# Hybrid decoder trunk on one core: a fourth query buffer, other background rates, weight conversion in instructions of 1,024 columns

## The chip, the core and the metric

The kernel runs on one core of one Trainium2 chip. A core has five engines that matter here: TensorE (PE) multiplies matrices into PSUM, VectorE (DVE) and ScalarE (ACT) do element-wise work, GpSimd (POOL) does element-wise work in SBUF, and SyncE (SP) issues most of the DMAs. Each engine takes its own instructions in order; engines wait for each other through semaphores. The metric is the device time of one execution in microseconds, as the median of several runs. Before the change it was 1137.51 us (three runs, 1137.13 to 1138.04).

## What is computed

A decoder trunk of two layers over 512 tokens with 1,024 features: a gated short convolution and an MLP, then one shared key/value projection, then native sparse attention with 16 heads in four groups, and a second MLP. What the change touches is the attention:

```python
def nsa_attention(q, gates, k_cmp, v_cmp, k_sel, v_sel, k_win, v_win, rel_bias):
    ...
    def one_block(qb):                     # 4 blocks of 128 queries
        ...
        logit_c = einsum('bqghd,bngd->bqghn', qt, k_cmp) + bias_c      # 31 compressed keys
        p_c = softmax(where(valid_c, logit_c, NEG_INF)) * has_any
        o_c = einsum('bqghn,bngd->bqghd', p_c, v_cmp)
        ...
        logit_s = einsum('bqghd,bqgkd->bqghk', qt, ks) + bias_s        # selected keys
        o_s = einsum('bqghk,bqgkd->bqghd', softmax(logit_s), vs)
        ...
        logit_w = einsum('bqghd,bkgd->bqghk', qt, kw) + bias_w         # window keys
        o_w = einsum('bqghk,bkgd->bqghd', softmax(logit_w), vw)
        o = gt[..., 0:1] * o_c + gt[..., 1:2] * o_s + gt[..., 2:3] * o_w
```

With 512 tokens the selection takes all eight blocks of 64 keys and the window covers all 512 keys, so both branches attend to all earlier keys. The compressed keys and values come from a small MLP ("phi") over overlapping blocks of 32 tokens.

## The kernel before

All matrices are worked on as 16-bit pairs (a high and a low part), so each product is three matmuls (`mm3`, L341 to L343). Weights come from memory in 32 bit, in pieces of up to 1,024 columns on 128 partitions. `load_piece` issues the DMA of a piece on SP's queue into one of three staging tiles `wst`; `convert_piece` (L171) makes the high part `whi` on ScalarE (L195) and the low part `wlo` on VectorE (L196); `next_piece` takes a piece for use and converts it at once if nobody has. Two pieces are kept converted ahead of the one in use. `convert_piece` has a parameter `step`: with its default of 1,024 a piece is one instruction on each engine, with 512 it is two. In the attention stage `ahead_fine` (L671) calls it with 512 and hands out one half at a time, between the matmuls of a projection.

The attention stage first makes keys, values, gates and the queries of group 0 in one go. Then it runs a list of 96 items. A `Full` item is one group of heads, one block of 128 queries and one branch, with four heads in the first query block, two in the second and one in the third and fourth; 22 items make a head group. A `Cmp` item is the compressed branch of two groups and one query block. Items 0 to 21 belong to group 0, 22 to 43 to group 1, 44 to 69 to group 2 with four `Cmp` items among them (54, 57, 60 and 63), 70 to 95 to group 3 with the other four. An item has five parts which run in later and later steps of the loop, so that several items are under way:

- `st0`: logits on TensorE (L953, L954; L1023, L1024 for `Cmp`), bias and row minimum on VectorE (L961), exponential on ScalarE (L963)
- `st1`, two steps later: transposes on TensorE (L969), high part on ScalarE (L972)
- `st2`, three steps later: low part on VectorE (L975)
- `st3`, four steps later: product with the values (L988 to L990), scaling on VectorE (L906), sums on GpSimd (L908, L911)
- `st4`, six steps later: where a query block is complete, transposes of the output (L922) and its split into the tile `big`

Beside the items runs a generator, `background`, which makes in this order: `raw(0)` (raw keys for phi), `queries(1)`, `phi(0)`, `raw(1)`, `queries(2)`, `phi(1)`, `queries(3)`, and then `out_proj(0)`, the first half of the output projection, once groups 0 and 1 are finished. Each unit is three matmuls of 512 columns (credit 0.65) or six of 155 columns (credit 0.42). In each step of the item loop a credit is added, and units are taken until the credit is used up; a unit of no declared credit counts 0.1. Where an item needs something that is not made yet (`need`), the generator is first run on until it is. What is left over after the last item is run at the end, followed by `out_proj(2)`, the second half, and the second MLP.

A projection accumulates in two PSUM banks `a` (`gated_pair`); `phi` holds the same two banks until its own epilogue has read them. `queries(g)` ends with two multiplications on VectorE into the buffers `at_s` (three, shared with the items' logits), four copies on ScalarE (L742) and four subtractions on GpSimd (L743), which make the tile `Q` of four heads. There are three `Q` tiles, and `queries(3)` writes where group 0 was read; since item 63 is the last reader of group 0, `queries(3)` holds its allocation back until that item has been issued (`cmp0`). `raw` writes its result into `big` by twelve DMAs on SP's queue (L767 to L769).

The program's order on each engine is not quite the order of these calls: the framework orders instructions by its own estimates when it builds the program.

Of the kernel before, what the change touches and what calls it, by code (L numbers as in the profile page):

```python
# [11 lines left out]
F16 = mybir.dt.float16  # L12
# [8 lines left out]
S, D, F, H, G, DH = 512, 1024, 4096, 16, 4, 64  # L21
# [27 lines left out]
def body(ctx, tc, x, rel_bias, norm_mix, norm_mlp, mlp_w1, mlp_w2, a_w_in, a_conv_w, a_w_out,  # L49
# [15 lines left out]
    def bank(tag, shape=(128, 512)):  # L65
        n = {"a": 2, "b": 2, "c": 2, "d": 1, "e": 1}[tag]
        return psum.tile(list(shape), F32, name=tag, bufs=n)
# [78 lines left out]
    def blocked(i):  # L146
        return pieces[i][1] is None
# [23 lines left out]
    def convert_piece(step=1024):  # L171

        i = pos["cv"]
        if i >= len(pieces):
            return
        _, shape, sc = pieces[i]
        t = staged.pop(i)
        pos["cv"] += 1
        if shape is None:
            b = t.rearrange("p (k b n) -> p k b n", k=2, n=128)  # L180
            for e, o, x, y in W_SUMS:
                DVE.tensor_tensor(b[:, :, o], b[:, :, x], b[:, :, y], op=e)  # L182
            hi, lo = (wk[0].tile([128, 2, 7, 128], F16, name=n, bufs=NW2) for n in ("whi2", "wlo2"))
            ACT.activation(hi, b[:, :, 1:], AF.Copy, scale=sc)  # L184
            DVE.scalar_tensor_tensor(lo, b[:, :, 1:], sc, hi, op0=OP.mult, op1=OP.subtract)  # L185
            ready[i] = (hi, lo)
            yield
        else:
            a, n = shape
            hi = wpool.tile([128, PIECE], F16, name="whi", bufs=NW)  # L190
            lo = wpool.tile([128, PIECE], F16, name="wlo", bufs=NW)
            for s in range(0, a * n, step):
                e = min(s + step, a * n)
                w = t[:, s:e]
                ACT.activation(hi[:, s:e], w, AF.Copy, scale=sc)  # L195
                DVE.scalar_tensor_tensor(lo[:, s:e], w, sc, hi[:, s:e], op0=OP.mult, op1=OP.subtract)  # L196
                yield
            r = lambda w: w[:, :a * n].rearrange("p (a n) -> p a n", a=a)
            ready[i] = (r(hi), r(lo))
        while pos["dma"] < len(pieces):  # L200
            like = [j for j in range(pos["cv"], pos["dma"]) if blocked(j) == blocked(pos["dma"])]
            if len(like) >= (NS2 if blocked(pos["dma"]) else NS):
                break
            load_piece()
# [153 lines left out]
    def ftile(name, bufs=2, n=S):  # L358
        return wk[0].tile([128, n], F32, name=name, bufs=bufs)
# [240 lines left out]
    with pool("attn") as ap:  # L600
# [42 lines left out]
        def scaled(ps, rb):  # L643
            t = ftile("at_s", 3)
            DVE.tensor_tensor(t, ps, rb, op=OP.mult)
            return t
# [23 lines left out]

        def ahead_fine():  # L671
            while pos["cv"] < min(pos["use"] + AHEAD, len(pieces)):
                yield from convert_piece(512)


        def keys(br):
# [54 lines left out]

        def queries(g):
            po = yield from gated_pair(xq)
            while g == 3 and "cmp0" not in done:
                yield "wait"
            q = ap.tile([128, 4, S], F16, name="Q", bufs=3)
            for m in range(2):
                t = scaled(po[m], rbq)
                for s in range(2):
                    h, r = 2 * m + s, slice(64 * s, 64 * s + 64)  # L740
                    o = slice(64 - 64 * s, 128 - 64 * s)
                    ACT.activation(q[r, h], t[r], AF.Copy)  # L742
                    POOL.tensor_tensor(q[o, h], t[r], q[r, h], op=OP.subtract)  # L743
                yield
            Qs[g] = q
# [94 lines left out]
        done = set()  # L840
# [40 lines left out]
        for k in (keys(0), keys(1), marked("q0", queries(0)), values(0), values(1), gates()):  # L881
            drain(k)
# [123 lines left out]
        class Cmp:  # L1006
# [7 lines left out]

            def st0(self):
                gp, qb, n = self.gp, self.qb, self.n
                if (gp, qb) == (0, 3):
                    done.add("cmp0")
                s = bank("b")[:, 0:256].rearrange("p (h n) -> p h n", h=8)
                for j in range(8):  # L1020
                    g, h = 2 * gp + j // 4, j % 4
                    q = Qs[g][:, h, qb * 128:(qb + 1) * 128]
                    PE.matmul(s[:, j, :n], q, KC[:, 0, g, :n], start=True, stop=False)  # L1023
                    PE.matmul(s[:, j, :n], q, KC[:, 1, g, :n], start=False, stop=True)  # L1024
                lg = ftile("at_s", 3)[:, 0:256].rearrange("p (h n) -> p h n", h=8)
                i = 8 * qb + 7
                tc_ = TC[gp].rearrange("p g h n -> p (g h) n")
                tv = tc_[:, :, i::-1] if i - n < 0 else tc_[:, :, i:i - n:-1]
                DVE.tensor_tensor(lg[:, :, :n], s[:, :, :n], tv, op=OP.add)
                mx = ap.tile([128, 8], F32, name="c_m", bufs=2)  # L1030
                DVE.tensor_reduce(mx, lg[:, :, :n], axis=mybir.AxisListType.X, op=OP.max)
                DVE.tensor_tensor(lg[:, :, :n], lg[:, :, :n], mx[:, :, None].to_broadcast([128, 8, n]),
                                  op=OP.subtract)
                self.p = ftile("at_p", 3)[:, 0:256].rearrange("p (h n) -> p h n", h=8)
                if n < 32:
                    POOL.memset(self.p[:, :, n:], 0.0)
                ACT.activation(self.p[:, :, :n], lg[:, :, :n], AF.Exp, bias=zero, scale=1.0 / SL)
                self.l = ap.tile([128, 8], F32, name="c_l", bufs=4)
                DVE.tensor_reduce(self.l, self.p[:, :, :n], axis=mybir.AxisListType.X, op=OP.add)
# [76 lines left out]
        credit = 3.0  # L1116
        for i in range(len(items) + 6):
            if i < len(items):
                for k in items[i].need():
                    while k not in done:  # L1120
                        if next(bg, "end") in ("wait", "end"):
                            raise RuntimeError(k)
                at_item.get(i, lambda: None)()
                items[i].st0()
            credit += 0.91 if i < 54 else 0.72 if i < 68 else 0.6
            while credit > 0.0:
                u = next(bg, "end")
                if u in ("wait", "end"):
                    credit = 0.0
                else:  # L1130
                    credit -= u or 0.1
            for s in (1, 2, 3, 4):
                j = i - lead[s]
                if 0 <= j < len(items):
                    getattr(items[j], f"st{s}")()
# [9 lines left out]
    with pool("hidden_b") as hp:  # L1145
# [5 lines left out]
        for half in range(2):  # L1151
            nc.gpsimd.dma_start(fng[half], bass.AP(tensor=final_norm.tensor, offset=final_norm.offset + half * S,
                                                   ap=[[0, 128], [1, S]]))
# [130 lines left out]
```

## Time and profile before

| what | value |
|---|---|
| median of three runs | 1137.51 us |
| the profiled execution | 1136.88 us |
| its span, first to last instruction | 1135.1 us |
| TensorE busy | 1095.8 us, 97% of the span |
| VectorE busy | 832.3 us, 73% |
| ScalarE busy | 568.5 us, 50% |
| GpSimd busy | 157.6 us, 14% |
| mean granted TensorE clock | 0.995 |

A row of a group reads: line of the kernel, engine, operation, output and inputs with their shapes, how often, then busy time in microseconds and the mean duration in nanoseconds, then the idle time of the engine before such instructions and what ended it. A row of the timeline reads: start and duration in microseconds, engine, line, operation, and in brackets the idle time before it and what released it. Matmuls overlap in these records, so the cost of one on a busy TensorE is the distance between two starts, not its duration.

### The profile page before, as it was taken

How to read it: one execution, taken by the hardware profiler on the slowest of the kernel's cores; microseconds unless marked ns; L12 is line 12 of the kernel's file. 1: busy time of each engine (PE TensorE's matmuls, PEld its weight loads, DVE VectorE, ACT ScalarE, POOL GpSimd, SP SyncE). 2: the span in 40 equal slices, each digit the busy share in tenths (PEclk: the TensorE clock that was granted, in tenths of full speed). 3: DMA queues.
4: the chain of work that ended last, by engine and by line, in shares of the span. 5: the costliest groups of instructions: out<-in, count | busy, mean ns of one | idle time of the engine just before them, and what ended most of it. 6: DMA issues, size and time to landing. Idle time of an engine off the chain costs nothing.

```text
span 1135.1 us, 20099 instructions
## 1 busy us (share of the span) xinstructions
PE 1095.8 (97%) x7959; PEld 694.1 (61%) x7959; DVE 832.3 (73%) x1498; ACT 568.5 (50%) x922; POOL 157.6 (14%) x198
## 2 busy tenths in 40 slices
PE   8999999999999999999999989899999999999985
PEld 4444444446884448865767666664444787445874
DVE  4755458765897556999589969896895598754795
ACT  4532235444433444556679777765544433343452
POOL 0000000422000221001002022220122100123020
PEclk9999999999999999999999999999999999999998
DMA  6433335333333333313334341112633333330221
GB/s 210 130 94 97 107 105 172 113 93 113 112 112 112 111 95 107 112 42 120 112 78 122 83 138 38 39 38 74 187 111 112 111 109 115 105 95 7 84 84 75
DMA packets 149378, 115.75 MB, mean 102 GB/s; under 512 B 8612, under 2 KB 146564, under 8 KB 149284
## 3 DMA queue, kind: packets, MB, share of 16 engines
q1 hardware_dynamic: 146736, 109.47, 31.8%
q10 hardware_dynamic: 2260, 4.40, 1.3%
q8 instruction: 62, 1.02, 0.4%
q0 software_dynamic: 288, 0.61, 0.2%
q14 instruction: 32, 0.26, 0.1%
HBM read 110.22 MB, written 2.14 MB: 99 GB/s over the span
## 4 chain that ended last, share of the span: by engine, by line
PE 50%; DVE 19%; ACT 11%; issue 7%; POOL 7%; DMA 5%; SPq 1%; DVEq 0%; ACTq 0%; POOLq 0%
POOL ml_z L503 6%; PE a L341 4%; PE a L342 4%; PE a L343 4%; DVE wlo L185 4%; DMA wst<-mlp_w_dram 3%; ACT rh L504 3%; PE c L343 3%; PE c L342 3%; PE c L341 3%; PE b L342 3%; PE b L341 3%; PE b L343 3%; DVE wlo L196 3%; DVE ml_t L499 2%
## 5 line engine op out<-in xcount | busy, mean ns | idle before, releaser
L195 ACT ACTIVATE whi<-wst 128x1024 f16<-128x1024 f32 (+4 forms) x171 | 142.4, 858 | 127.9 <-PE b L342 38.4
L196 DVE SCALAR_TENSOR_TENSOR wlo<-wst,whi 128x1024 f16<-128x1024 f32 (+4 forms) x171 | 169.9, 1001 | 40.2 <-ACT whi L195 39.9
L503 POOL TENSOR_TENSOR ml_z<-ml_z 128x256 f32<-128x256 f32 x128 | 99.9, 801 | 610.1 <-ACT ml_z L501 410.1
L184 ACT ACTIVATE whi<-wst 128x1792 f16<-128x1792 f32 x64 | 106.9, 1692 | 135.4 <-DVE wst L182 102.3
L341 PEld LDWEIGHTS <-whi 128*128 128x128 f16 x1024 | 100.4, 98 | 112.3 <-issue 5.5
L343 PEld LDWEIGHTS <-wlo 128*128 128x128 f16 x1024 | 100.2, 98 | 112.1 <-issue 0.4
L342 PEld LDWEIGHTS <-whi 128*128 128x128 f16 x1024 | 100.2, 98 | 107.6 <-issue 2.0
L505 DVE TENSOR_TENSOR rl<-ml_z,rh 128x1792 f16<-128x1792 f32 x32 | 64.8, 2026 | 135.9 <-ACT rh L504 135.7
L185 DVE SCALAR_TENSOR_TENSOR wlo<-wst,whi 128x1792 f16<-128x1792 f32 x64 | 128.8, 2019 | 3.0 <-ACT whi L184 2.9
L182 DVE TENSOR_TENSOR wst<-wst 128x256 f32<-128x256 f32 x256 | 108.9, 469 | 24.4 <-DMA wst<-mlp_w_dram 23.4
L504 ACT ACTIVATE rh<-ml_z 128x1792 f16<-128x1792 f32 x32 | 54.3, 1698 | 106.1 <-POOL ml_z L503 106.1
L551 PEld LDWEIGHTS <-whi 128*128 128x128 f16 x896 | 87.7, 98 | 16.2 <-issue 5.6
L552 PEld LDWEIGHTS <-wlo 128*128 128x128 f16 x896 | 87.6, 98 | 15.0 <-issue 4.2
L550 PEld LDWEIGHTS <-whi 128*128 128x128 f16 x896 | 87.7, 98 | 10.5
L343 PE MATMUL b<-xsh,wlo 128*128 128x512 f16 x208 | 78.8, 379 | 0.0
L342 PE MATMUL b<-xsl,whi 128*128 128x512 f16 x208 | 78.8, 379 | 0.0
L341 PE MATMUL b<-xsh,whi 128*128 128x512 f16 x208 | 78.7, 379 | 0.0
L501 ACT ACTIVATE ml_z<-ml_t 128x1024 f32<-128x1024 f32 x32 | 33.8, 1057 | 88.4 <-DVE ml_t L499 88.4
L963 ACT ACTIVATE at_p<-at_s,at_m 128x128 f32<-128x128 f32 (+3 forms) x128 | 71.0, 557 | 13.7 <-DVE at_m L961 12.6
L551 PE MATMUL a<-rl,whi 128*128 128x256 f16 x256 | 69.8, 273 | 3.7 <-DVE rl L505 3.7
L341 PE MATMUL c<-xsh,whi 128*128 128x512 f16 x192 | 72.8, 379 | 0.0
L342 PE MATMUL c<-xsl,whi 128*128 128x512 f16 x192 | 72.8, 379 | 0.0
(309 smaller groups left out, 2686.4 us busy)
## 6 DMA issues: line engine op xcount, KB each, us to landing
wst<-mlp_w_dram SPq DMA_DIRECT2D x256, 256.0 KB, 3.3
wst<-a_w_in_dram SPq DMA_DIRECT2D x18, 512.0 KB, 3.5
wst<-w_kv_dram SPq DMA_DIRECT2D x12, 512.0 KB, 3.5
T<-ext_d ACTq DMA_DIRECT2D x4, 1056.0 KB, 6.0
wst<-a_w_out_dram SPq DMA_DIRECT2D x8, 512.0 KB, 3.4
wst<-b_w_qg_dram SPq DMA_DIRECT2D x8, 512.0 KB, 3.5
wst<-b_w_o_dram SPq DMA_DIRECT2D x8, 512.0 KB, 3.3
wst<-a_w_in_dram SPq DMA_DIRECT2D x8, 384.0 KB, 5.5
```

The source lines that it names most:

```text
L182: DVE.tensor_tensor(b[:, :, o], b[:, :, x], b[:, :, y], op=e)
L184: ACT.activation(hi, b[:, :, 1:], AF.Copy, scale=sc)
L185: DVE.scalar_tensor_tensor(lo, b[:, :, 1:], sc, hi, op0=OP.mult, op1=OP.subtract)
L195: ACT.activation(hi[:, s:e], w, AF.Copy, scale=sc)
L196: DVE.scalar_tensor_tensor(lo[:, s:e], w, sc, hi[:, s:e], op0=OP.mult, op1=OP.subtract)
L341: PE.matmul(ps, w[0], xs[0], start=start, stop=False)
L342: PE.matmul(ps, w[0], xs[1], start=False, stop=False)
L343: PE.matmul(ps, w[1], xs[0], start=False, stop=stop)
L503: POOL.tensor_tensor(z[:, o], z[:, a], z[:, b], op=e)
L504: ACT.activation(rh[0][:, p], z[:, 1:8], AF.Copy)
L550: PE.matmul(acc7[i], wh, xh, start=c == 0 and not other, stop=False, skip_group_check=other)
L551: PE.matmul(acc7[i], wh, xl, start=False, stop=False, skip_group_check=other)
```

## The change

Three things change in the attention stage. There are four `Q` tiles instead of three, and the hold of `queries(3)` until item 63 is gone. `ahead_fine` converts a piece of 1,024 columns in one instruction on each engine instead of two. The credit of each step is set by another table: 1.04 for steps 0 to 41, 0.65 for 42 to 52, 0.68 for 53 to 68 and 0.74 from 69, where it was 0.91 up to step 53, 0.72 up to 67 and 0.6 from 68.

```diff
         def ahead_fine():
             while pos["cv"] < min(pos["use"] + AHEAD, len(pieces)):
-                yield from convert_piece(512)
+                yield from convert_piece()
...
         def queries(g):
             po = yield from gated_pair(xq)
-            while g == 3 and "cmp0" not in done:
-                yield "wait"
-            q = ap.tile([128, 4, S], F16, name="Q", bufs=3)
+            q = ap.tile([128, 4, S], F16, name="Q", bufs=4)
...
             def st0(self):
                 gp, qb, n = self.gp, self.qb, self.n
-                if (gp, qb) == (0, 3):
-                    done.add("cmp0")
...
-            credit += 0.91 if i < 54 else 0.72 if i < 68 else 0.6
+            credit += 1.04 if i < 42 else 0.65 if i < 53 else 0.68 if i < 69 else 0.74
```

## The prediction

> **What bounds the kernel now.** I read the page's first part, then busy time in windows, then TensorE's waits, then single rows.
>
> ```profile
> span 1135.1 us, 20099 instructions
> PE 1095.8 (97%) x7959; PEld 694.1 (61%) x7959; DVE 832.3 (73%) x1498; ACT 568.5 (50%) x922; POOL 157.6 (14%) x198
> ```
>
> TensorE is the bound of the whole, so the change can only win where TensorE waits. All edits act in the attention stage. I cut it where the timeline shows the first logits matmul (L953, L1023) of items 0, 22, 44, 63, 72 and 95, up to the next MLP at 797 us.
>
> ```profile
> 555.10:601.70 46.60, 45.62 (x460) 31.04 (x457) 38.02 (x111) 38.90 (x103) 6.12 (x7) 1.00 0.29 81
> 601.70:659.70 58.00, 53.84 (x577) 37.04 (x573) 49.06 (x140) 44.68 (x125) 5.80 (x7) 1.00 0.46 131
> 659.70:699.70 40.00, 37.85 (x507) 29.38 (x505) 35.37 (x120) 31.47 (x97) 8.18 (x10) 1.00 0.25 81
> 699.70:719.90 20.20, 16.36 (x181) 12.16 (x177) 17.71 (x49) 14.41 (x32) 9.16 (x8) 0.92 0.00 1
> 719.90:765.40 45.50, 44.93 (x519) 32.38 (x517) 44.28 (x136) 33.80 (x98) 7.61 (x11) 1.00 0.15 48
> 765.40:797.00 31.60, 30.57 (x205) 15.56 (x202) 22.65 (x40) 16.23 (x30) 3.01 (x5) 1.00 0.23 67
> ```
>
> After the window come its length, then busy time (and instructions) of PE, PEld, DVE, ACT and POOL, then the granted clock and the DMAs. TensorE idles 1.0, 4.2, 2.2, 3.8, 0.6 and 1.0 us in the six, 12.7 us together: a change can win about one per cent. The stage from 719.9 is tight on VectorE too (44.28 of 45.5 us); the tail from 765.4 is TensorE alone.
>
> ```profile
> PE b L953 <- POOL Q L743: 2.5, 5, 0.6
> PE b L953 <- DVE at_m L961: 2.1, 3, 1.2
> PE a L341 <- DMA big<-kr_hl: 2.1, 1, 2.1
> PE c L969 <- DVE at_pl L975: 2.0, 4, 1.0
> PE c L922 <- POOL o L911: 1.5, 2, 0.9
> ```
>
> These are TensorE's waits from 560 to 780 us (total, times, longest). Each head group begins with a wait for Q, whose last step is GpSimd's subtraction (L743). How long that takes after the last query matmul is read from single rows:
>
> ```profile
> 595.34 0.38 PE L343 MATMUL a<-xqh,wlo 128*128 128x512 f16 x1
> 602.78 0.23 PE L953 MATMUL b<-KD,Q 128*128 128x128 f16 x1 [0.61 <-POOL Q L743]
> ...
> 655.91 0.38 PE L343 MATMUL a<-xqh,wlo 128*128 128x512 f16 x1
> 658.57 0.23 PE L341 MATMUL a<-big,whi 128*128 128x155 f16 x1 [2.06 <-DMA big<-kr_hl]
> 662.91 0.23 PE L953 MATMUL b<-KD,Q 128*128 128x128 f16 x1 [0.62 <-POOL Q L743]
> ...
> 705.70 0.38 PE L343 MATMUL a<-xqh,wlo 128*128 128x512 f16 x1
> 713.77 0.23 PE L953 MATMUL b<-KD,Q 128*128 128x128 f16 x1 [0.49 <-POOL Q L743]
> ```
>
> From the group's last query matmul to the last head's first product: 7.4, 7.0 and 8.1 us. Whatever TensorE work does not fill that time is lost. The third loss also costs clock:
>
> ```profile
> 710.00:715.00 5.00, 2.23 (x20) 1.26 (x18) 3.71 (x9) 3.58 (x8) 3.49 (x4) 0.97 0.00 2
> 715.00:720.00 5.00, 4.91 (x61) 4.76 (x62) 4.29 (x15) 3.28 (x9) 1.27 (x1) 0.69 0.01 3
> ```
>
> After five microseconds with TensorE busy 2.23, the granted clock was 0.69 for the next five: 5 x 0.31 = 1.6 us lost.
>
> **The change part by part.** *Fourth Q buffer and the dropped gate: 0.* Walking the loop by its credits, item 63 opens the gate in its own step, and the matmuls of queries(3) end only in step 65. The gate holds nothing, and the buffer freed by item 63 is free two steps before it is rewritten. The cover is those two steps; without it the price would be one more wait like the 0.6 us of L953 on Q.
>
> *Rates.* The units of background are the same; only their steps move. The same walk gives: Q of group 1 done in step 17 instead of 19; before item 44, 5 pieces of queries(2) forced ahead instead of 12; phi(1) done by force at item 54 (5 yields, four of them empty) instead of in step 52; Q of group 3 in step 68 instead of 66; after item 95's own step no unit left instead of 2. Counting L341 to L343 in the order of both programs gives what moves between the windows (512-column and 155-column matmuls, before to after; a piece of weights feeds 24): items 0 to 21, 96 and 30 to 96 and 72; 22 to 43, 96 and 82 to 96 and 52; 44 to 71, 48 and 84 to 57 and 72; 72 to 94, 72 to 78; after item 95's logits, 120 to 105. Their prices are the distances of starts:
>
> ```profile
> 700.09 0.38 PE L341 MATMUL a<-xqh,whi 128*128 128x512 f16 x1
> 700.31 0.38 PE L342 MATMUL a<-xql,whi 128*128 128x512 f16 x1
> ...
> 599.49 0.23 PE L342 MATMUL a<-big,whi 128*128 128x155 f16 x1
> 599.56 0.23 PE L343 MATMUL a<-big,wlo 128*128 128x155 f16 x1
> ```
>
> 0.216 and 0.07 us (below, work by starts means such distances, each taken where nothing waits), so +2.9, -2.1, +1.1, +1.3 and -3.2 us.
>
> *Conversion in one instruction.*
>
> ```profile
> L195 ACT ACTIVATE whi<-wst 128x1024 f16<-128x1024 f32 x92 | 94.4, 1049 | 102.2 <-PE b L342 38.4 <-PE c L342 30.8 <-PE a L342 22.3
> L195 ACT ACTIVATE whi<-wst 128x512 f16<-128x512 f32 x68 | 40.2, 623 | 15.4 <-PE a L342 12.2 <-PE b L702 2.5 <-PE e L831 0.5
> L196 DVE SCALAR_TENSOR_TENSOR wlo<-wst,whi 128x1024 f16<-128x1024 f32 x92 | 112.2, 1220 | 29.6 <-ACT whi L195 29.4
> L196 DVE SCALAR_TENSOR_TENSOR wlo<-wst,whi 128x512 f16<-128x512 f32 x68 | 49.1, 738 | 2.7 <-ACT whi L195 2.6
> ```
>
> A pair of halves costs VectorE 2 x 738 - 1220 = 256 ns more, ScalarE 2 x 623 - 1049 = 197 ns. The 68 halves become 34 instructions: 8.7 and 6.7 us less work, but most of it under TensorE. It counts where these engines are full, and there the page Perfetto Trace Analysis of the Trainium skill (section Optimizing Scalar/DVE Operations) speaks for it: larger operations help a saturated engine. The same section speaks against it elsewhere: where the engine is not full but makes others wait, splitting lets work finish sooner. VectorE is at 82% and 85% in the first two windows, so by that rule the sum there would lose the gain of the merge and add the delays of the first rival below.
>
> Now the sum, window by window.
>
> Items 0 to 21: +2.9 moved in, of which 0.5 fits into the 1.0 us idle: **+2.4** (+1.9 to +2.9).
>
> Items 22 to 43: -2.1 moved out. The wait at 602.78 goes (-0.6): 11.7 us of TensorE work by starts stand between Q's last matmul and item 22 instead of 5.3, more than the 7.4 us that Q takes. For group 2, 3.8 us of work instead of 1.9 stand inside the 7.0 us, so -1.9. The DMA wait of 2.06 us is inside this: its copies are issued late, behind raw(1) that ended in step 39, at 0.6 us each on SP's queue.
>
> ```profile
> 650.46 0.60 SPq L767 DMA_DIRECT2D big<-kr_hl  x1
> 653.74 0.60 SPq L769 DMA_DIRECT2D big<-kr_hl  x1
> ...
> 605.00:625.00 20.00, 19.06 (x243) 14.86 (x241) 18.23 (x63) 19.24 (x64) 1.46 (x2) 1.00 0.51 161
> ```
>
> raw(1) now ends in step 34, five steps of 2.6 us (58.0 / 22) sooner, with all its twelve copies; of the weight loads on that queue only the small second phi weight changes its place among them. So the wait is gone; what is late next is Q, already counted. From 605 to 625 us ScalarE is busy 19.24 of 20 us; the window's 178 / 24 = 7.4 pieces give 2.6 to those 20 us, x 197 ns: -0.5. Against it, phi(0) now ends at items 23 and 24: its two banks are held by its epilogue, the next projection cannot start, and the items that must fill in are two-head ones with more ScalarE work. I take +0.6, like a wait of L953 on Q; bounds 0 and 3.2, the TensorE work by starts that stands there without any projection. Together **-4.5** (-6.3, all 4.2 of idle and the 2.1 moved, to +0.3, with 3.2 and neither Q gain).
>
> Items 44 to 71: +1.1 moved in. For group 3, 6.5 us of work instead of 4.6 inside 8.1 us: -1.9. The clock loss of 1.6 I halve, since idle of 1.6 us remains there: -0.8. VectorE is busy 53.1 of 60.2 us and saves 132 / 24 = 5.5 pieces x 256 ns = 1.4, half of it seen: -0.7. The five forced yields at item 54 cost 0: that item's st3, which needs VC, comes four steps later. Together **-2.3** (-6.5, all 6.0 of idle and the 1.6 of clock less 1.1, to +2.6: the 1.1 in full, Q3 one step of 60.2 / 28 = 2.2 us later against item 70, and 0.7 of merge).
>
> Items 72 to 94: +1.3 moved in, against 3 pieces x 256 ns = 0.8 off a full VectorE and 0.6 us idle: **0** (-0.8 to +1.3).
>
> From item 95: 15 matmuls fewer where TensorE alone works: **-3.2** (-4.1 with a wait on L911 of 0.9 us gone too, -2.3 if VectorE's last residuals then set the end).
>
> The conversions outside these windows lie ahead of item 0, beside the keys and values, and in the tail, where TensorE has its own work: 0.
>
> Sum: 2.4 - 4.5 - 2.3 + 0 - 3.2 = -7.6 us. The profiled execution took 1136.88 us (span 1135.1 and 1.78 around it), 0.63 below the median of 1137.51 and 0.25 below the lowest run shown. It would become 1129.3; I forecast the median, **1129.9 us**, with its own range of 1126 to 1135.
>
> **The rivals.** *Slower: whole conversions hold up the softmax chain.* Place: VectorE and ScalarE, in order, between st0 and st1.
>
> ```profile
> L961 DVE CUSTOM_DVE_ANT_0 at_s<-b,T 128x512 f32<-128x512 f32 x32 | 21.8, 681 | 2.9 <-POOL Q L743 1.7 <-PE b L954 1.0
> L963 ACT ACTIVATE at_p<-at_s,at_m 128x512 f32<-128x512 f32 x32 | 23.0, 717 | 4.5 <-DVE at_m L961 3.7 <-DVE rlc L1066 0.6
> ```
>
> The chain is 0.68 + 0.72 = 1.4 us of the two steps (46.6 / 22 = 2.1 us each) before st1 needs it. A conversion ahead on both engines now adds 1.22 + 1.05 = 2.3 us, and 0.5 is left; before, a half added 1.4. One more operation of 0.7 us in that place breaks it. Price per piece: (1.22 - 0.74) + (1.05 - 0.62) = 0.9 us. The windows use (126 + 178 + 132 + 72) / 24 = 21 pieces; it decides from (7.6 + 2.3) / 0.9 = 11 pieces that show in full, and two thirds of them, 14, cost 12.6 against -7.6: 1142.5 us. For it: L969 already waits on L975. Against it: those waits sum to 2.0 us in 220.
>
> *The stalls only change places.* The moved work shows in full (+2.9), phi(0)'s end costs its 3.2 (+0.3), Q3 is late (+2.6), and only VectorE's 0.8 and the tail's 3.2 come back: 2.9 + 0.3 + 2.6 - 0.8 - 3.2 = +1.8, 1139.3 us. For it: every group switch has had its wait. Against it: the order has more work under each Q.
>
> *All idle is filled.* The low ends sum to 1.9 - 6.3 - 6.5 - 0.8 - 4.1 = -15.8; all at once is unlikely, seven tenths of it gives 1126.4 us.
>
> *The change does nothing it says*, for the buffer: that is my own case above, worth 0 in all cases.
>
> **How the numbers follow.** Forecast 0.58, all idle filled 0.10, places changed 0.13, slower 0.19. The range of 8 in 10 leaves out the far halves of the outer cases: 1125.0 to 1140.0. A measurement of this kernel tells 0.2% (2.3 us) from no change. Faster takes the forecast and the idle case, 0.68; same the third, 0.13; slower 0.19.
>
> **What would show it.** Right: in the tail window some 3 us less from item 95 to the next MLP; no wait of L341 on the copies into big; the L953 waits on Q shorter for groups 1 and 2; VectorE's L196 all at 128x1024 with 1.22 us. Wrong: L969 or L953 waiting on VectorE for over 5 us in all (the chain); a granted clock under 1.00 in a second place, or an idle stretch of 3 us behind phi(0).

## The result and the profile after

The changed kernel takes 1144.32 us (median of six, 1142.09 to 1146.55); the kernel before 1137.04 us (six, 1135.42 to 1138.04). The ratio is 1.0064 with an interval of 1.0051 to 1.0077: 7 us slower, where 7.6 us faster was forecast. The profiled execution took 1144.84 us with a span of 1142.8, so 7.7 us more of span than before.

The first part of the page of the changed kernel, span and busy times:

```profile
span 1142.8 us, 20031 instructions
...
PE 1100.7 (96%) x7959; PEld 695.7 (61%) x7959; DVE 828.6 (73%) x1464; ACT 565.9 (50%) x888; POOL 155.9 (14%) x198
```

The same 7959 matmuls; VectorE has 34 instructions less and is busy 3.7 us less, ScalarE 34 and 2.6 us. The groups of the changed kernel's conversions, by shape:

```profile
L196 DVE SCALAR_TENSOR_TENSOR wlo<-wst,whi 128x1024 f16<-128x1024 f32 x126 | 155.5, 1236 | 36.6 <-ACT whi L195 36.4
L195 ACT ACTIVATE whi<-wst 128x1024 f16<-128x1024 f32 x126 | 129.7, 1048 | 113.3 <-PE b L342 38.1 <-PE c L342 32.5 <-PE a L342 26.5
```

No 512-column form is left, and 126 is 92 and the 34 pairs. So the merge did what it says. Where the time went stands in the windows of the changed kernel, cut at the first logits of items 0, 22, 44, 63, 72 and 95 and at the next MLP (length, then busy time of PE, PEld, DVE, ACT, POOL, then the clock):

```profile
555.40:606.00 50.60, 48.67 (x502) 33.71 (x499) 41.04 (x111) 40.92 (x101) 6.93 (x7) 1.00 0.34 96
606.00:665.60 59.60, 53.67 (x567) 37.08 (x564) 45.84 (x128) 41.56 (x114) 4.67 (x6) 0.97 0.38 110
665.60:704.60 39.00, 35.42 (x461) 26.17 (x457) 35.40 (x111) 30.04 (x90) 6.91 (x10) 1.00 0.23 71
704.60:733.70 29.10, 21.73 (x218) 15.26 (x216) 21.72 (x65) 19.04 (x47) 9.99 (x8) 0.88 0.10 34
733.70:779.00 45.30, 44.72 (x508) 31.84 (x505) 43.45 (x123) 31.21 (x84) 7.11 (x11) 1.00 0.15 48
779.00:808.10 29.10, 27.63 (x191) 14.24 (x187) 21.13 (x35) 15.61 (x27) 3.48 (x5) 1.00 0.26 75
```

Against the windows of before: +4.0, +1.6, -1.0, +8.9, -0.2 and, with the tail of before taken up to the MLP's first matmul at 797.2 (31.8 us), -2.7 us. The second MLP behind them takes 334.7 us instead of 337.9, and item 0 begins 0.3 us later; the sum is +7.7. The fourth window, items 63 to 71, is the loss: TensorE idles 7.4 of its 29.1 us and the clock is 0.88. The second window has a clock of 0.97, which before had 1.00. TensorE's waits of the changed kernel from 560 to 780 us (total, times, longest):

```profile
PE b L951 <- POOL Q L741: 7.5, 6, 3.5
PE b L951 <- DVE at_m L959: 5.0, 5, 2.2
PE c L967 <- DVE at_pl L973: 1.7, 2, 1.1
```

(L951, L959, L967, L973, L740 and L741 are L953, L961, L969, L975, L742 and L743 of the kernel before.) The logits wait 7.5 us for `Q` where they waited 2.5, and 5.0 us for a row minimum where they waited 2.1.

**The last queries.** The timeline of the changed kernel around `queries(3)`:

```profile
711.88 0.38 PE L343 MATMUL a<-xqh,wlo 128*128 128x512 f16 x1
...
719.03 0.68 DVE L645 TENSOR_TENSOR at_s<-a,rb 128x512 f32<-128x512 f32 x1
...
720.23 0.68 DVE L645 TENSOR_TENSOR at_s<-a,rb 128x512 f32<-128x512 f32 x1
720.37 2.57 ACT L740 ACTIVATE Q<-at_s 64x512 f16<-64x512 f32 x4
...
721.73 5.69 POOL L741 TENSOR_TENSOR Q<-at_s,Q 64x512 f16<-64x512 f32 x4
...
722.94 0.23 PE L951 MATMUL b<-KD,Q 128*128 128x128 f16 x1 [3.54 <-POOL Q L741]
...
727.48 0.28 PE L951 MATMUL b<-KD,Q 128*128 128x128 f16 x1 [0.83 <-POOL Q L741]
```

The same two scalings in the kernel before, whose last matmul of these queries began at 705.70:

```profile
706.16 0.69 DVE L645 TENSOR_TENSOR at_s<-a,rb 128x512 f32<-128x512 f32 x1
...
708.57 0.69 DVE L645 TENSOR_TENSOR at_s<-a,rb 128x512 f32<-128x512 f32 x1
```

Before, the chain to `Q` began 0.5 us behind the matmul; now 7.2 us behind it. No row shows a wait at L645: it stands there in VectorE's order, behind the softmax of the items. The generator's turn that issues it comes a step of the loop later; that is a part of the reason and not all of it, since e7 below takes that turn out and 4.5 of the 7.2 us remain. Nothing else on TensorE is left by then, and the clock follows, in two windows of the changed kernel:

```profile
618.30:621.70 3.40, 3.40 (x15) 1.72 (x14) 2.08 (x9) 2.02 (x7) 0.00 (x0) 0.50 0.00 0
724.10:730.90 6.80, 4.21 (x32) 3.08 (x33) 1.65 (x10) 2.47 (x9) 3.17 (x3) 0.50 0.24 77
```

**The table.** The first of these two has another cause. The timeline of the changed kernel behind `phi(0)`:

```profile
607.95 0.37 ACTq L623 DMA_DIRECT2D T<-ext_d  x1
...
617.00 0.28 DVE L628 COPY Tc<-T 128x128 f32<-128x128 f32 x1 [2.30 <-DMA T<-ext_d]
...
618.01 0.32 PE L951 MATMUL b<-KD,Q 128*128 128x384 f16 x1 [2.25 <-DVE at_m L959]
618.17 0.41 PE L952 MATMUL b<-KD,Q 128*128 128x384 f16 x1
618.38 0.64 PE L341 MATMUL a<-xsh,whi 128*128 128x512 f16 x1
618.80 0.63 PE L342 MATMUL a<-xsl,whi 128*128 128x512 f16 x1
```

and the same copy in the kernel before, which waits for nothing:

```profile
601.87 0.37 ACTq L623 DMA_DIRECT2D T<-ext_d  x1
608.52 0.26 DVE L628 COPY Tc<-T 128x128 f32<-128x128 f32 x1
```

`T` is the table of biases of one head group; a small part of it is copied for the compressed branch (`load_T`). The copy is not wanted until item 74, the first compressed item of groups 2 and 3, but it stands in VectorE's order, and everything behind it stands too: the row minimum, and then TensorE, which has no projection to run there. Neither the conversions alone (e1 below) nor the rates alone (e2) make this stall: in both the table has landed when VectorE comes to the copy, at 623.20 and 614.75 us.

### The profile page after: what moved, and what is told of

Its sections match the earlier page's. It is cut to its first block, busy times and chain, and to the rows that moved or that the text cites. A ratio compares the mean times of both kernels' runs of the same rounds, so it can differ in the third digit from the quotient of the medians.

```text
span 1142.8 us, 20031 instructions
## 1 busy us (share of the span) xinstructions
PE 1100.7 (96%) x7959; PEld 695.7 (61%) x7959; DVE 828.6 (73%) x1464; ACT 565.9 (50%) x888; POOL 155.9 (14%) x198
## 5 line engine op out<-in xcount | busy, mean ns | idle before, releaser
L195 ACT ACTIVATE whi<-wst 128x1024 f16<-128x1024 f32 (+1 forms) x137 | 137.5, 1021 | 120.7 <-PE b L342 38.1
L196 DVE SCALAR_TENSOR_TENSOR wlo<-wst,whi 128x1024 f16<-128x1024 f32 (+1 forms) x137 | 164.4, 1201 | 44.7 <-ACT whi L195 44.5
L182 DVE TENSOR_TENSOR wst<-wst 128x256 f32<-128x256 f32 x256 | 105.4, 453 | 24.0 <-DMA wst<-mlp_w_dram 22.8
L961 ACT ACTIVATE at_p<-at_s,at_m 128x128 f32<-128x128 f32 (+3 forms) x128 | 70.8, 554 | 25.1 <-DVE at_m L959 24.5
L343 PE MATMUL c<-xsh,wlo 128*128 128x512 f16 x192 | 72.8, 379 | 0.0
```

Source lines behind the costliest of these rows:

```text
L343: PE.matmul(ps, w[1], xs[0], start=False, stop=stop)
```

## The experiments

All ratios are to the kernel before, run on the same chip, with a 95% interval. "Lost" is the length of a window less TensorE's work by starts (512 columns 0.216 us, 155 columns 0.07 us, and the distances of starts of the other shapes likewise). The windows of the profiled executions, in us, length and in brackets lost:

```
items              0-21        22-43       44-62       63-71       72-94       95-MLP      MLP
before             46.6 (1.7)  58.1 (6.7)  40.0 (4.5)  20.2 (6.9)  45.5 (1.9)  31.8 (1.8)  337.9
after              50.6 (2.8)  59.5 (9.4)  39.0 (6.4)  29.1 (11.4) 45.3 (1.6)  29.1 (2.3)  334.7
e1_merge           48.0 (3.1)  59.5 (7.7)  41.1 (6.0)  18.2 (4.9)  46.0 (2.5)  31.7 (1.6)  335.3
e2_rates           49.9 (2.0)  55.4 (4.9)  38.5 (6.6)  30.2 (12.1) 45.4 (1.7)  29.2 (2.4)  339.0
e3_q3early         50.6 (2.8)  61.2 (11.0) 39.1 (6.4)  21.1 (6.5)  49.1 (2.3)  29.1 (2.3)  334.8
e4_three           50.6 (2.8)  57.8 (7.7)  39.1 (6.4)  29.3 (11.7) 45.3 (1.6)  29.1 (2.3)  335.5
e5_oldhead         48.0 (3.1)  59.5 (7.7)  41.1 (5.9)  18.2 (4.9)  49.1 (2.3)  29.1 (2.3)  337.1
e7_q3tail          50.6 (2.8)  60.0 (9.8)  39.1 (6.4)  22.9 (8.4)  48.7 (1.9)  29.1 (2.3)  335.6
e8_tablepool       50.6 (2.8)  55.5 (5.3)  39.5 (6.9)  29.4 (11.8) 45.3 (1.6)  29.1 (2.3)  335.3
e9_both            50.6 (2.8)  55.5 (5.3)  39.5 (6.9)  23.0 (8.5)  48.5 (1.7)  29.1 (2.3)  335.5
e11_table_q66      50.6 (2.8)  55.5 (5.3)  41.0 (8.4)  22.0 (7.5)  48.7 (1.9)  29.1 (2.3)  335.6
e12_rates_q66      49.9 (2.0)  55.4 (4.9)  38.5 (6.6)  22.9 (7.9)  48.8 (2.0)  29.2 (2.4)  340.1
e13_rate84         49.9 (2.1)  54.9 (6.7)  44.2 (7.8)  18.1 (5.4)  47.0 (3.4)  32.2 (2.2)  338.4
b1_best            46.6 (1.7)  58.8 (7.4)  40.0 (4.5)  20.9 (7.5)  45.0 (1.4)  31.7 (1.6)  335.2
```

Each row is one execution, and a window differs between executions of the same order of instructions. e4 has the order of the changed kernel on every engine, e3 and e7 have it up to item 63; items 22 to 43 take 59.5 us in the changed kernel and 57.8, 61.2 and 60.0 us in these. In e4 the clock stays at 1.00 there:

```profile
605.60:663.40 57.80, 51.93 (x565) 36.26 (x562) 45.73 (x128) 41.42 (x114) 4.59 (x6) 1.00 0.39 113
```

What an edit is worth is therefore read from the ratios; the windows say where.

### Which of the three parts loses

e1 is the kernel before with whole conversions alone, e2 the kernel before with the new rates alone, e4 the changed kernel with three buffers and the gate.

```diff
e1, to the kernel before
-                yield from convert_piece(512)
+                yield from convert_piece()
e2, to the kernel before
-            credit += 0.91 if i < 54 else 0.72 if i < 68 else 0.6
+            credit += 1.04 if i < 42 else 0.65 if i < 53 else 0.68 if i < 69 else 0.74
e4, to the changed kernel
-            q = ap.tile([128, 4, S], F16, name="Q", bufs=4)
+            while g == 3 and "cmp0" not in done:
+                yield "wait"
+            q = ap.tile([128, 4, S], F16, name="Q", bufs=3)
...
+                if (gp, qb) == (0, 3):
+                    done.add("cmp0")
```

> The kernel before with whole conversions alone (rates, gate and three Q tiles as before). If whole conversions hold up the softmax chain, this alone is slower: 1.003 to 1.006 of before. If the loss comes from where the rates put the background, this is no slower: 0.997 to 1.001, since VectorE and ScalarE only have less work.

> The kernel before with the new rates alone (conversion in halves, gate and three Q tiles as before). If the rates carry the loss, 1.004 to 1.008 of before, with the long wait of TensorE on Q of group 3 ahead of item 70 still there (3 us or more) and the tail after item 95 some 5 us shorter. If whole conversions carry it, 0.996 to 1.001.

> The changed kernel with three buffers for queries and the gate on the last queries, as before; rates and conversions are the new ones. The instructions of every engine come out in the same order as in the changed kernel. Theory (the fourth buffer and the missing gate are worth nothing, since three buffers are not yet full when the last queries are made): the time of the changed kernel, 1.005 to 1.008 of the kernel before. Rival (the fourth buffer moves memory or waits): 1.003 or less, or 1.010 or more.

Measured: e1 1.0003 (0.9994 to 1.0012), e2 1.0057 (1.0044 to 1.0070), e4 1.0054 (1.0041 to 1.0067). All three lie in the ranges given for the rates as the cause and the buffer as nothing. The rates carry the loss, the conversions alone lose nothing in sum, and the buffer with its gate is worth nothing. One expectation failed: the tail of e2 is 2.6 us shorter and not some 5.

That e1 comes to zero is not that it does nothing. Its windows, of items 0 to 21, 22 to 43, 44 to 62 and 63 to 71:

```profile
554.70:602.70 48.00, 46.06 (x462) 31.11 (x458) 39.05 (x107) 39.19 (x100) 6.13 (x6) 1.00 0.30 82
602.70:662.20 59.50, 54.12 (x589) 37.80 (x586) 48.83 (x133) 44.57 (x117) 6.71 (x8) 1.00 0.45 126
662.20:703.30 41.10, 38.96 (x492) 29.79 (x491) 35.77 (x117) 30.53 (x93) 7.16 (x10) 0.96 0.24 78
703.30:721.50 18.20, 15.14 (x180) 11.01 (x176) 16.43 (x46) 14.27 (x31) 9.15 (x8) 1.00 0.00 1
```

Items 0 to 43 take 2.8 us more than before; TensorE's waits there for a row minimum (L961) and a low part (L975) rise from 1.0 to 2.5 us. Of the two windows behind them the one is 1.1 us longer and the other 2.0 us shorter. The stretch of halved clock has moved from the second to the first (0.96 of 41.1 us; before it was 0.92 of 20.2), but it does not set their length: e5, with the same order of instructions up to item 72, takes as long at a clock of 1.00:

```profile
661.40:702.50 41.10, 37.91 (x496) 28.84 (x493) 35.78 (x117) 30.59 (x93) 7.14 (x10) 1.00 0.24 77
702.50:720.70 18.20, 15.12 (x179) 10.99 (x176) 16.42 (x46) 14.27 (x32) 9.14 (x8) 1.00 0.01 2
```

The second MLP is 2.6 us shorter. Those of its waits that differ by more than 0.3 us, in the kernel before and then in e1:

```profile
PE a L551 <- DVE rl L505: 1.8, 1, 1.8
...
PE e L312 <- DVE rs_r L305: 0.9, 1, 0.9
PE a L1166 <- DVE X L531: 0.6, 1, 0.6
```

```profile
PE a L551 <- DVE rl L505: 0.4, 1, 0.4
```

In the profiles of this study the thirteen kernels with whole conversions at the end have an MLP of 334.3 to 337.1 us, the six with halves 337.1 to 340.1. Why an MLP that is itself unchanged waits less was not tried further.

The page Perfetto Trace Analysis of the Trainium skill (section Optimizing Scalar/DVE Operations) says that larger operations can help where an engine is saturated and that smaller ones may help where it is not but makes others wait. The trace agrees with the second half, at 2.8 us in items 0 to 43, where VectorE is busy 82% of the time in e1. It does not show the first: items 72 to 94, where VectorE was busy 97% of the time before, take 46.0 us in place of 45.5.

### Late queries

e3 makes the last queries in full in step 66; e7 only leaves out the generator's turns between their last matmul and their two scalings.

```diff
e3, to the changed kernel
+            while i == 66 and "q3" not in done:
+                next(bg)
             while credit > 0.0:
e7, to the changed kernel (no turn behind the last matmul and between the scalings, group 3)
-                        yield 0.65
+                        if tail or (half, c, m) != (1, 3, 1):
+                            yield 0.65
...
-            po = yield from gated_pair(xq)
+            po = yield from gated_pair(xq, tail=g < 3)
...
-                yield
+                if g < 3 or m == 1:
+                    yield
```

> The changed kernel, with queries(3) run to its end in step 66 instead of 68. If the loss around item 70 comes from Q's scaling standing two steps later on VectorE, 6 to 9 us come back: 0.998 to 1.001 of before, and the window of items 63 to 71 takes 20 to 23 us instead of 29. If whole conversions carry it, the time stays at 1.005 to 1.007.

> The changed kernel with the two scalings of the last queries (L645) issued in the step of their last matmul: the turn of the generator behind that matmul and the one between the halves are left out for group 3; no background matmul is held back for it. Theory of the late chain (what costs 9 us in items 63 to 71 is that the scalings stand 7 us behind the last matmul in VectorE's order): items 63 to 71 fall from 29.1 us to 21 to 24, items 72 to 94 stay at 45 to 47 because about as many background matmuls (20) stand in 63 to 71, and the time is 0.994 to 0.999 of the kernel before. Rival (the work is the cost: 20 background matmuls where 9 stood, and the start of the chain only moves the stall): items 63 to 71 stay above 27, or what they lose comes back in 72 to 94 as it half did when Q3 was forced in step 66, and the time is 1.002 to 1.006.

Measured: e3 1.0027 (1.0017 to 1.0037), e7 1.0048 (1.0035 to 1.0060). Items 63 to 71 and 72 to 94 of e3, then of e7:

```profile
705.90:727.00 21.10, 16.84 (x191) 11.94 (x189) 18.23 (x54) 15.99 (x37) 9.15 (x8) 1.00 0.07 22
727.00:776.10 49.10, 48.11 (x535) 33.90 (x531) 46.93 (x134) 33.78 (x94) 7.08 (x11) 1.00 0.17 54
```

```profile
705.60:728.50 22.90, 18.18 (x191) 12.97 (x190) 19.07 (x54) 16.41 (x39) 9.15 (x8) 0.93 0.06 21
728.50:777.20 48.70, 47.99 (x535) 33.93 (x532) 46.14 (x133) 33.40 (x92) 7.05 (x11) 1.00 0.18 55
```

The window of the stall falls from 29.1 us by 8.0 and 6.2, and the next rises from 45.3 by 3.8 and 3.4: nine background matmuls of 512 columns have gone from the one to the other (20 to 11 and 78 to 87), 1.9 us by starts, and that stretch, with TensorE busy 44.72 of its 45.3 us, has no idle time to take them. So in e3 the late queries cost 4.2 us net, in the profile (70.2 us for both windows, not 74.4) as in the ratio (0.0037). Beside other edits the same turn gives less: 0.0026 from e8 to e11 and 0.0019 from e2 to e12 below. Their share is a third of the loss or more, and in the changed kernel itself somewhat over half. The ratio of e3 lies between its two ranges, that of e7 in the range of its rival, which said that about half of what the window gains comes back in items 72 to 94, and so it does (3.4 of 6.2 us). In e7 the scalings moved less than meant: in VectorE's order they still stood 4.5 us behind the last matmul, and what puts them there was not traced; the framework puts instructions in order by its own estimates.

### The table

e8 has GpSimd make the copies of the tables of groups 2 and 3; the order of everything else is that of the changed kernel. e9 joins it with e7, e11 with e3. b3 is the same edit in the kernel before.

```diff
-            DVE.tensor_copy(TC[g // 2][:, g % 2], t[:, :, 0:512:16])
+            (POOL if g > 1 else DVE).tensor_copy(TC[g // 2][:, g % 2], t[:, :, 0:512:16])
```

> The changed kernel with the copies of the tables of groups 2 and 3 (Tc from T, L628) made by GpSimd in place of VectorE; the order of everything else on every engine is the same. Theory of the table (behind phi(0) VectorE stands 2.3 us at the copy until the table's transfer has landed, the row minimum behind it is late and TensorE idles 2.25 us, and the clock halves for 3.4 us): items 22 to 43 fall from 59.5 us to 55 to 57, the clock record near 618 us is gone, and the time is 1.002 to 1.004 of the kernel before. Rival (whole conversions on VectorE and ScalarE hold up the row minimum there, the copy is only what stands in front): TensorE still waits 2 us or more there, items 22 to 43 stay above 58, and the time is 1.005 to 1.007.

> The changed kernel with both edits: scalings of the last queries in the step of their last matmul, and the table's copy on GpSimd. Theory of two places (late queries and the late table together make the loss): the two gains add, and the time is 0.990 to 0.996 of the kernel before. Rival (one stall covers the other, or the loss lies elsewhere): 0.999 or more.

> The kernel before with the tables of groups 2 and 3 copied by GpSimd, and nothing else. In the kernel before VectorE stands 3.1 us at such a copy, but TensorE waits only 0.6 us for a row minimum in items 22 to 43, so if the stall matters only where a row minimum stands behind it, the time is 0.998 to 1.001; if every such stall of VectorE costs TensorE its length, 0.996 to 0.998.

Measured: e8 1.0043 (1.0029 to 1.0057), e9 1.0018 (1.0008 to 1.0029), b3 0.9998 (0.9990 to 1.0007). Items 22 to 43 of e8, and then GpSimd's timeline there:

```profile
605.30:660.70 55.40, 51.73 (x564) 36.27 (x561) 45.48 (x127) 41.47 (x114) 4.99 (x7) 1.00 0.41 118
```

```profile
615.30 0.40 POOL L628 COPY Tc<-T 128x128 f32<-128x128 f32 x1 [12.39 <-DMA T<-ext_d]
```

The window falls from 59.6 to 55.4 us and its clock is 1.00 again. The conversions, which were the rival, stand where they stood, so they are not the cause. The 4.2 us of this profile hold a halved clock that e4 did not have, and from e4's window it is 2.4 us. The ratios give 0.0021 or 2.4 us, about a third of the loss; from e7 to e9 the same edit gives 0.0030, from e3 to e11 0.0010. The same kind of stall costs the kernel before nothing, although VectorE stands there once for longer, as its timeline shows:

```profile
656.07 0.28 DVE L628 COPY Tc<-T 128x128 f32<-128x128 f32 x1 [3.13 <-DMA T<-ext_d]
```

There TensorE runs the last matmuls of `queries(2)` to 656.4 us and then waits 2.06 us for the DMAs into `big` in any case; at 617 us of the changed kernel it has nothing but logits left. e8 is just above its range. e9 missed its range and lies in its rival's; the two gains do add (0.0046, alone 0.0016 and 0.0021), but a rest of 2 us stays. e7 moves the chain only part of the way, so some of that rest may still be the late queries.

### The rest

e10 is e2 with the edit of e7, e12 is e2 with the edit of e3. e5 is the changed kernel with the old rates up to step 67 and the new one behind, e13 the kernel before with the new rate only up to step 41 and a higher one after that:

```diff
e5, to the changed kernel
-            credit += 1.04 if i < 42 else 0.65 if i < 53 else 0.68 if i < 69 else 0.74
+            credit += 0.91 if i < 54 else 0.72 if i < 68 else 0.74
e13, to the kernel before
-            credit += 0.91 if i < 54 else 0.72 if i < 68 else 0.6
+            credit += 1.04 if i < 42 else 0.84 if i < 68 else 0.6
```

> The changed kernel with the old rates up to step 67 and 0.74 from 68. If head rates carry the whole loss (phi(0)'s end and Q of group 3), it keeps only the gain behind item 72: 0.994 to 0.998 of before. If whole conversions carry it, 1.002 or more.

> The kernel before with the new rates alone (which took 1.0057) and the scalings of the last queries in the step of their last matmul. Theory of the late chain: with halves there is no stall at the table, so the late queries are all that the rates lose; items 63 to 71 fall from 30.2 us to 22 to 25, and the time is 0.997 to 1.001. Rival (the work is the cost): 1.003 to 1.006.

> The changed kernel with the tables of groups 2 and 3 copied by GpSimd and the last queries made in full in step 66. The two edits gave 2.9 us and 4 us when made alone. Theory (the late table and the late queries are the whole loss; the table's copy behind the queries' scaling only left a part of it): 0.997 to 1.001, items 22 to 43 at 55 to 56 us, items 63 to 94 together at 70 to 71. Rival (a third loss): 1.003 or more.

> The kernel before with the new rates, halves as before, and the last queries made in full in step 66. Theory (the rates lose by the late queries alone; moving the scalings by one step left 2 us of the wait for the queries in place): 0.998 to 1.002. Rival (the rates lose elsewhere too, since the edit with the scalings gave only 2 us of 7): 1.003 to 1.005.

> The kernel before, halves as before, with the new rate 1.04 for the first 42 items, then 0.84 up to item 68 and 0.6 behind it. The last queries' scalings then stand at the same place of VectorE's order as before or one row earlier, without being forced. Theory (the new rates lose by their low rates from item 42 on: the last queries come late, and in items 44 to 62 TensorE is left without background work to fill the chain of the softmax, 6.6 us lost where 4.5 were): items 44 to 62 lose no more than 5 us, items 63 to 94 together take 66 to 68 us, and the time is 0.997 to 1.001. Rival (the high rate ahead of item 42 is what loses): 1.003 or more.

Measured: e5 1.0003 (0.9994 to 1.0011), e10 1.0040 (1.0028 to 1.0053), e11 1.0017 (1.0009 to 1.0026), e12 1.0038 (1.0024 to 1.0052), e13 1.0042 (1.0029 to 1.0054). Only e11 comes near its range; the others missed theirs on the slow side, and e10, e12 and e13 lie where their rivals had them.

e5 says that the whole loss is in the rates of steps 0 to 67, and that the new last rate is worth nothing: the tail is 2.7 us shorter, and items 72 to 94 are longer by the same work (49.1 against 46.0 us in e1).

e11 says that the late queries and the table are most of the loss of the changed kernel and not all of it: 0.0017 of 0.0064 is left. Of the loss of the rates beside halves, where there is no stall at this table, e12 takes back only a third (1.0057 to 1.0038). Where the rest may lie is seen in items 44 to 62 of e2, beside the third window of before (40.00 us, PE 37.85, DVE 35.37):

```profile
660.90:699.40 38.50, 34.66 (x451) 25.94 (x448) 35.10 (x114) 30.48 (x95) 6.56 (x10) 1.00 0.23 74
```

3.6 us of TensorE's work by starts left this stretch, and it became 1.5 us shorter. Half of the 3.6 is background (35 and 70 matmuls of 512 and 155 columns where 39 and 84 were); the other half is products of the items themselves, of which 1.0 us now stands ahead of the first logits of item 44 and the rest behind those of item 63. VectorE's work did not move: 35.1 of 38.5 us. Items 0 to 21, which took 42 of the matmuls of 155 columns, are TensorE's (48.67 of 50.60 us in the changed kernel) and pay for all of them. That this is the rest is argued from the windows, not shown: e13, which gave the work back to items 44 to 62, lost 7.8 us there and not less. Its trace shows a clock halved for 6.8 us in that window, and waits of the logits for `Q` of 2.6 us where they were 1.4:

```profile
659.60:703.80 44.20, 41.30 (x507) 32.10 (x508) 37.07 (x119) 33.03 (x100) 8.48 (x10) 0.92 0.31 97
```

e13's rival, the high rate ahead of item 42, is not the cause by itself: items 0 to 21 lose 3.3 us and items 22 to 43 gain 3.2, and b5 below has the same rates and is not slower than the kernel before.

### What might beat both

b2 is the kernel before with whole conversions only from the end of `phi(1)` on; b1 has the table's copy on GpSimd too. b4 is e12 with both, b5 is e13 with both.

```diff
-                yield from convert_piece(512)
+                yield from convert_piece(*([] if "cmp" in done else [512]))
```

> The kernel before with its own rates, whole conversions only from the end of phi(1) on (halves until then), and the tables of groups 2 and 3 copied by GpSimd. Theory (whole conversions cost about 4 us in items 0 to 62 and give 2 us in items 63 to 71 and 2 to 3 us in the second MLP; the table's copy on VectorE costs a stall): 0.993 to 0.997. Rival (what whole conversions give late is tied to what they cost early, so that the end is the same): 0.999 to 1.001.

> The kernel before with whole conversions only from the end of phi(1) on, and nothing else. Theory (the gain of whole conversions lies behind item 63): 0.994 to 0.998. Rival (tied to the early cost): 0.999 to 1.001.

> The kernel of the experiment before this one, with whole conversions from the end of phi(1) on and the two tables copied by GpSimd. Theory (late whole conversions give what they gave beside the old rates, with the tables about 0.0016): 0.996 to 1.000. Rival (the new rates have no cover left for them): 1.002 or more.

> The kernel of the experiment before this one, with whole conversions from the end of phi(1) on and the tables of groups 2 and 3 copied by GpSimd. Theory: 0.995 to 0.999, about 0.002 below it. Rival (the high rate ahead of item 42 is what loses): 1.001 or more.

Measured: b1 0.9984 (0.9975 to 0.9994), b2 0.9994 (0.9984 to 1.0003), b4 1.0000 (0.9991 to 1.0009), b5 0.9991 (0.9982 to 1.0000). b1 is faster than the kernel before, though by less than 0.2%, and b2 and b3 do not tell which of its edits gives it. b1 and b2 missed their ranges, and b2 lies in its rival's: in the profile of b1 the MLP is 2.7 us shorter, as hoped, but items 63 to 71 are not (20.9 us, 7.5 of them lost). b4 and b5 stand 0.0038 and 0.0051 below the kernels that they are made from, twice to three times what the same two edits give beside the old rates (0.0016). b4 is at the edge of its range and b5 just above. Which of the two edits gives it beside the new rates was not taken apart.

## Why the prediction was wrong

- *Items 0 to 21, +2.4.* Right in kind, +4.0: 2.9 moved in, and of the rest 0.8 is the merge (2.8 lost in the changed kernel, 2.0 in e2). The 0.5 us that was to fit into idle time did not.
- *Items 22 to 43, -4.5.* The 2.1 us moved out and the two gains were there in part: the DMA wait of 2.06 us is gone, and without the table the window is 55.4 us, -2.6. What failed is the term "+0.6, like a wait of L953 on Q; bounds 0 and 3.2" for the end of `phi(0)`. The place was right and the price was not: VectorE, not TensorE's fill, sets it, at the copy of a table that the sum did not know. By the ratios it is 2.4 us, four times the term and within its bounds; with the halved clock of the profiled execution it is 4.2, over the upper bound. The high end of this window, given as +0.3, comes to +0.6 by its own terms (-2.1 - 0.5 + 3.2); the second rival would be 1139.6 us by it.
- *Items 44 to 71, -2.3.* The windows give +7.9. This is the step that failed most: "For group 3, 6.5 us of work instead of 4.6 inside 8.1 us: -1.9". The 8.1 us were counted from the last matmul, as if the chain began there. It begins with the scaling, which has its own place in VectorE's order; from the last matmul to the last head's first product it took 15.6 us (711.88 to 727.48) in place of 8.1. Items 63 to 71 took 4.4 us more work by starts and 4.5 us more loss; e3 gave back 4.2, net of what went on into items 72 to 94. The sum's own high end had 2.2 us for queries one step late: the right danger, at half its price.
- *The merge, -0.5, -0.7 and -0.8 in three windows.* The price of a pair of halves was taken from durations, which overlap when instructions follow each other: 256 and 197 ns, 8.7 and 6.7 us in all. VectorE and ScalarE are busy 3.7 and 2.6 us less. In the kernel before, where VectorE does not wait, its next instruction starts 0.60 us after a half and 1.14 us after a whole one, so a pair costs 0.07 us more and not 0.26. The three terms were 2.0 us together, so this does not decide.
- *Items 72 to 94, 0, and the tail, -3.2.* -0.2 and -2.7: right. Luck helped the first: 1.1 us of the items' own products came to stand ahead of item 72. And e5 shows that the tail's gain is only work moved to items 72 to 94 and earlier, which pay it.
- *Rates as a zero sum of moved work.* The count took the items' own products to stay in their windows. Items 44 to 62 gave up 2.9 us of work, of which 1.3 is background, and became 1.0 us shorter; the rest is products that came to stand in the windows on both sides. VectorE's work there stayed as it was (35.40 us after, 35.37 before); that it holds the length is not shown.
- *Outside the windows, 0.* The second MLP gave 3.2 us, in the direction opposite to the result; why stays open.
- *Buffer and gate, 0.* Right (e4).
- *The rivals.* "Whole conversions hold up the softmax chain" named the right sign and nearly the time, and its mechanism is not the cause: e1 is 1.0003. That its 1142.5 us lie near the measured 1144.3 is luck. Its sign is in the profile as well: L951 and L967 (L953 and L969 before) wait 6.7 us for VectorE where the limit was 5, but 2.25 of it stand behind the table's copy. "The stalls only change places" named both true places, late queries and the end of `phi(0)`, and sized both too small. Of what was to show it, the halved clock in a second place is in the profile (618.3 and 724.1); the idle stretch behind `phi(0)` is 2.25 us and not 3, and the one of 3.5 us stands at the last queries. The signs of being right are there too: the tail, the DMA wait and the conversions came out as said. They told where stalls would go, and none told where new ones would come.

## What to carry to other kernels

A wait for a chain of small operations is counted from the place of its first operation in its own engine's order, not from the end of the work that feeds it; when a rate or a credit is changed, look first at which turn issues that operation. Before work is moved between stretches at its price on one engine, see whether that engine sets the length of both: what leaves a stretch that another engine holds may not be returned (here argued from items 44 to 62, not shown). A copy that is wanted late and waits for a transfer stalls all that stands behind it in the order, and in these runs it cost time only where TensorE had nothing to cover it. Here two changes that do not make the stall when each is alone made it together. And what one execution's window shows of an edit is checked against a second execution of the same order before it is given a price.

## What the runs showed of the hardware

- The clock halves without a full stretch of idle: in the changed kernel it went to 0.50 at 618.3 behind a wait of 2.25 us and the short products around it, with TensorE busy 1.15 of the 3.4 us before. The starts of 512-column matmuls then stand 0.42 us apart (618.38 and 618.80) in place of 0.216. It does not always follow: in e4, with the same order and a wait of 2.19 us in the same place, the clock stayed at 1.00. The page TensorE: Matmul & The Clock Gate of the Trainium skill (section What's actually happening) has the clock fall after an idle window of about 3.4 us and rise after a busy one of that length. The stretches at 0.50 here, 3.4 and 6.8 us, agree with one and two such windows; that a whole idle window is needed is not what the row at 618.01 shows.
- The same transfer of a table, 1,056 KB, landed 6 us after its issue in the kernel before and 9.0 us after it in the changed one. There two loads of the weights of `phi(1)`, which come earlier by the new rates, were issued on SP's queue, the first 0.8 us ahead of it, as its timeline shows; that they slow it is not shown:

```profile
607.19 2.71 SPq L167 DMA_DIRECT2D wst<-phi_v_w_dram  x2
```

The transfer in the kernel before and in the changed one, as windows from issue to landing (the last two columns are the share of the DMA engines and GB/s):

```profile
601.90:607.90 6.00, 5.39 (x89) 5.15 (x87) 5.23 (x29) 4.72 (x20) 0.82 (x1) 1.00 0.79 228
```

```profile
608.00:617.00 9.00, 6.29 (x84) 5.28 (x85) 6.56 (x33) 6.64 (x29) 0.00 (x0) 1.00 0.86 281
```
